# Ten of the sixteen S5 kernel matrices laid out in rows during the attention heads instead of during the S5

## The chip, the cores and the metric

One NeuronCore of a Trainium2 chip runs the whole program. The metric is device time in microseconds (us) of one execution, the median of several. Five engines work side by side, each through its own list of instructions and strictly in that list's order: TensorE (PE; PEld is its weight load), VectorE (DVE), ScalarE (ACT), GpSimd (POOL) and SyncE (SP). SP, ACT and POOL also issue DMAs, which share 16 DMA engines.

## The reference, cut to what matters

Two blocks on 256 tokens of width 1024: the first has an MLA attention layer and an S5 layer, the second two more attentions and a gated convolution. In the S5 layer 128 groups of 16 channels each pass through a linear recurrence, in both directions, over 256 context and 256 latent tokens:

```
def _s5_direction(u_ctx, u_lat, lam, dt, bmat, cmat):
    lam_bar = jnp.exp(lam * dt[:, None])
    b_bar = ((lam_bar - 1.0) / lam)[..., None] * bmat
    ...
        bu = jnp.einsum('btgs,gps->btgp', u_chunk.astype(jnp.complex64), b_bar)
        _, xs = lax.associative_scan(_ssm_combine, (a, bu), axis=1)
        xs = xs + powers[None] * h[:, None]
        y = jnp.einsum('btgp,gsp->btgs', xs, cmat).real
```

What a token contributes to the outputs of its own neighbourhood of four tokens depends on lam, dt, bmat and cmat alone, and not on the activations.

## The kernel before, in words

Tokens are taken in 64 steps of four. Within a step of four, the S5 is one small matrix per group (a 64 x 64 block-Toeplitz matrix, 4 tokens by 16 channels on either side); from step to step a state is carried. The 128 groups are worked in 16 sub-blocks of 8 (`m` or `sb`, 0 to 15).

**Ahead of the S5.** `s5_pre` makes three things of each sub-block from the parameters: BTd (input to state), CCd (state to output) and Kd, the distinct 16 x 16 blocks of the small matrices. All three go to DRAM. Sub-blocks 0 to 9 (`S5_EARLY = 10`) are made during the first projections (`region1`), 10 to 15 during the MLA output projection (`mla_out`). `s5_toeplitz` (L1127 to L1136) then copies Kd to Td, DRAM to DRAM, so that each row of a small matrix lies in one piece: 8 DMAs from the POOL queue, in pieces of 64 numbers (256 bytes).

**The S5 itself** (`s5`) follows a plan written by hand (`S5_PLAN`). Its first part is `sums`. For each sub-block m it projects the inputs of sub-block m + 2 (`inputs`; ACT copies them to `Ub` at L1178, writes them to DRAM as ud at L1179, POOL reads them back as `U` at L1185), and multiplies U with BTd on PE (`chunk_sums`, 64-partition matmuls, PSUM tiles `a`). ACT copies the products to `Sc` (L1214) and `s` (L1218). After every second sub-block DVE runs a tree over `Sc` (tiles `sc`, `Sc`), which gives the carried states of two sub-blocks, and between the trees the steps of a sequential scan (tiles `ss`, `s`). The tree of two sub-blocks is 24 DVE instructions, each scan 63 steps of three.

`direct(m)` is the part inside a step of four: SP loads the inputs (`Ul`, L1244) and the rows of the small matrices (`Ysb`, L1247, from Td; two buffers), ACT spreads Ysb into a zeroed matrix `x` (L1251, two copies; two such matrices, used in turn), and PE multiplies (`c` <- `Ul`, `x`, four matmuls of 64 columns). `outputs(m)` adds the part that comes from the states: ACT (or DVE) copies the states to `whi` (L1264 to L1271), PE multiplies into the same `c`. After every second sub-block ACT copies `c` to `Yb` (L1281) and writes it to DRAM as yd (L1282). `activate` reads four sub-blocks of yd back to `hl` (POOL, L1296), applies gelu (ACT, L1297), and `glu` multiplies by the first half of the GLU weights (PE, `a` <- `hl`, `raw`, L1311 loads). `gate` (PE, `b` <- `s`, `raw`; ACT, `sg`) is independent of the scans.

**What sets the order.** The program is written in Python, but a scheduler reorders it: it simulates the engines and puts each engine's instructions in an order of its own, within the dependences. A part written earlier, or made ready earlier, may move far. The list that results is fixed; on the chip each engine waits at its head.

The two places of the diff are `mla_heads`, which loops over the 16 heads, and `sums` in `s5`, where the Td writes are issued behind the read of U for m = 1 to 4:

```
if S5_LATE == 16 and m in TPM:
    with self.tc.issue_after(self.u_read):
        i = TPM.index(m)
        n = 8 // len(TPM)
        self.s5_toeplitz(0, 16, range(n * i, n * i + n))
```

Of the kernel before, what the change touches and what calls it, by code (L numbers as in the profile page):

```python
# [54 lines left out]
NR = 2  # L55
TPM = (1, 2, 3, 4)
TOEP = 0
ZGM = 6
PREM = (1, 1, 1, 1, 1, 1, 0, 0)
HLL = False  # L60
# [21 lines left out]
S5_EARLY = 10  # L82
# [125 lines left out]
class Builder:  # L208
# [380 lines left out]
    def mla_heads(self, rest):  # L589
# [48 lines left out]
        def scores(h):  # L638
            if h >= HM:
                return  # L640
            qa = st.pop(("qa", h))
            qf, qp = st.pop(("rot", h))
            pl = []

            def rotary(ps, x, q, keys, stop):

                self.mm(ps, x[:, q], self.kr[0][:, keys], False, False)
                self.mm(ps, x[:, q], self.kr[1][:, keys], False, stop)

            for tt in range(2):  # L650
                q = slice(tt * P, (tt + 1) * P)
                ps = self.ps("b")
                self.mm3(ps, two(qa, al, q), self.ckv, True, False)
                rotary(ps[:, lat], qp, q, lat, False)
                rotary(ps[:, cx], qf, q, cx, True)
                pl.append(self.softmax(att, ps, NT, MLA_SCALE, "pl", 4))
            ps = self.ps("b", (P, 2, NL))
            for tt in range(2):
                q = slice(NL + tt * P, NL + (tt + 1) * P)
                self.mm3(ps[:, tt], two(qa, al, q), two(self.ckv, al, cx), True, False)  # L660
                rotary(ps[:, tt], qf, q, cx, True)
            st["p", h] = pl, [self.softmax(att, ps[:, tt], NL, MLA_SCALE, "pc", 4) for tt in range(2)]

        def transposes(h):
            pl, pc = st.pop(("p", h))
            pt_l, pt_c = pair([P, 4, NL], "ptl", 1), pair([P, 2, NL], "ptc", 1)
            for b in range(2):
                pt = self.ps("c", (P, 2, 2, P))
                for k in range(2):
                    for tt in range(2):  # L670
                        nc.tensor.transpose(pt[:, k, tt], pl[tt][:, (2 * b + k) * P:(2 * b + k + 1) * P], self.ident)  # L671
                self.split(pt_l[0][:, 2 * b:2 * b + 2], pt_l[1][:, 2 * b:2 * b + 2], pt.rearrange("p k t q -> p k (t q)"))
            pt = self.ps("c", (P, 2, 2, P))
            for k in range(2):
                for tt in range(2):
                    nc.tensor.transpose(pt[:, k, tt], pc[tt][:, k * P:(k + 1) * P], self.ident)
            self.split(pt_c[0], pt_c[1], pt.rearrange("p k t q -> p k (t q)"))
            st["pt", h] = pt_l, pt_c

        def values(h):  # L680
            pt_l, pt_c = st.pop(("pt", h))
            po = self.ps("a")
            for k in range(4):
                self.mm3(po[:, lat], (self.V[0][:, k], self.V[1][:, k]), (pt_l[0][:, k], pt_l[1][:, k]), k == 0, k == 3)
            for k in range(2):
                self.mm3(po[:, cx], (self.V[0][:, 2 + k], self.V[1][:, 2 + k]), (pt_c[0][:, k], pt_c[1][:, k]), k == 0, k == 1)
            o = pair([P, NT], "o", 2)
            self.split(o[0], o[1], po)
            st["o", h] = o

        def outputs(h):
            if h < 0:
                return
            if h % 8 == 0:
                st["wuv"] = self.unit("w_uv", h // 8, 8, P)
                self.acts.append((self.s16([P, 8, NT], F32R), self.s16([P, 8, NT], F32R)))
            w = st["wuv"]
            pv = self.ps("a")
            self.mm3(pv, (w[0][:, h % 8], w[1][:, h % 8]), st.pop(("o", h)), True, True)
            g = self.gates[h // 8][:, h % 8]  # L700
            self.tt(g, pv, g, ALU.mult)
            a = self.acts[h // 8]
            self.split(a[0][:, h % 8], a[1][:, h % 8], g)
# [9 lines left out]
        for h in range(HM):  # L713
            scores(h + 1)
            if h == HM - 1 and FIRST_OUT == 0:
                self.out_first()
            transposes(h)
            queries(h + 2)
            if h == HM - 1 and FIRST_OUT == 1:
                self.out_first()  # L720
            values(h)
            outputs(h - 1)
            next(mods[h // 8])
        if FIRST_OUT == 2:
            self.out_first()
        outputs(HM - 1)
# [89 lines left out]
    def mla_out(self, pool):  # L816
# [18 lines left out]
        def scaled(kt):  # L835

            nc.scalar.activation(zG[:, kt, :NL], z[:, kt, :NL], AF.Copy, scale=G[:, kt, 0:1])
            nc.vector.tensor_scalar(zG[:, kt, NL:], z[:, kt, NL:], G[:, kt, 1:2], None, op0=ALU.mult)

        for m in range(KT):  # L840
# [10 lines left out]
            for _ in range(PREM[m]):  # L851
                next(bg, None)
            if m == ZGM:
                zG = self.s16([P, KT, NT])
                for kt in range(m):
                    scaled(kt)
            if m >= ZGM:
                scaled(m)
# [3 lines left out]
        zg = room.enter_context(pool("zg"))  # L862
        if TOEP:
            self.s5_toeplitz(0, TOEP)
        self.s5_steps(tmp)
# [273 lines left out]
    def s5(self):  # L1139
# [15 lines left out]
        def inputs(m, both=False):  # L1155

            if m in S5_SPLIT:
                ps = self.ps()
                if m == S5_SPLIT[0]:
                    hh.extend((self.s16([P, KT, NT], F32R), self.t(l1, [P, KT, NT], F32R, "hl", 1)))  # L1160
                    with self.tc.issue_after(self.h1_last):
                        for kt in range(KT):
                            x = self.split(hh[0][:, kt], hh[1][:, kt], self.h1[:, kt])
                    if HLL:
                        self.h_last = x
                self.linear(ps, "w_u", m, 1, KT, hh, al)
                place(m, ps)
            else:
                ms = range(m, m + 1 + both)
                ps = [self.ps() for _ in ms]  # L1170
                for x in self.linears32(ps, "w_u", ms, self.h1, al):
                    pass
                for i, p in zip(ms, ps):
                    place(i, p)
# [145 lines left out]
        def sums(m0, m1):  # L1320
            for m in range(m0, m1):
                if NR <= m + 2 < 16:
                    inputs(m + 2)
                for sb, at in LATE_AT:
                    if at == m:
                        if sb < 16:
                            next(bg)
                        else:
                            self.s5_toeplitz(TOEP, 16)
                if S5_LATE == 16 and m in TPM:  # L1330
                    with self.tc.issue_after(self.u_read):
                        i = TPM.index(m)
                        n = 8 // len(TPM)
                        self.s5_toeplitz(0, 16, range(n * i, n * i + n))
                yield from chunk_sums(m)

        def take(it, n=1):
# [3 lines left out]
        def turns(parts):  # L1341

            for k in range(3 * max([n for _, n in parts], default=0)):
                for blk, n in parts:
                    if k < 3 * n:
                        take(s[blk])
                        yield
# [16 lines left out]
        with ExitStack() as es:  # L1364
            for what, *x in S5_PLAN:
                if what == "order":
                    es.enter_context(self.in_order("p"))
                elif what in ("direct", "outputs", "gates", "y", "glu"):
                    if what == "y" and y32 is None:
                        y32 = self.t(l1, [P, 16, NL], F32, "hl", 1)  # L1370
                    if len(x) > 2:
                        glu(x[0], *x[2:])
                        continue
                    for m in range(*x):
                        dict(direct=direct, outputs=outputs, gates=gate, y=activate, glu=glu)[what](m)
                else:
                    steps = x[what == "sums":]
                    n, ops = turns(steps), 3 * sum(k for _, k in steps)
                    if what == "sums":
                        for i, _ in enumerate(sums(4 * x[0], 4 * x[0] + 4)):  # L1380
                            take(n, ops * (i + 1) // 48 - ops * i // 48)
                    take(n, 999)
# [475 lines left out]
```

## Time and profile before

| what | value |
| --- | --- |
| median of 3 runs | 1410.92 us (1406.25 to 1411.26) |
| profiled execution: its own time, its span | 1411.13 us, 1409.4 us |
| PE busy, DVE busy, ACT busy, POOL busy | 1346.1, 1056.6, 826.7, 88.6 us |
| mean granted TensorE clock | 0.981 |
| heads | about 160 to 380 us of the span |
| S5, `sums` to the first glu products | about 500 to 800 us |

The trace gives times from the start of the span. Each engine's timeline lists instructions with start and length, with runs of like ones merged; in square brackets stands how long the engine was idle before and what released it. PE's granted clock is a share of full speed: 1.00 is 2.4 GHz, 0.50 is 1.2 GHz. One matmul of four-byte numbers, such as those of `direct`, shows as two instructions on PE.

### The profile page before, as it was taken

The numbers are of one execution on the slowest core, as the hardware profiler recorded it, in microseconds if no ns is written. First come the engines' busy times: TensorE is split into PE (matmuls) and PEld (weight loads), VectorE is DVE, ScalarE is ACT, GpSimd is POOL, SyncE is SP. The second block draws the span as 40 slices with busy tenths as digits, with TensorE's granted clock in tenths as the row PEclk, the third lists the DMA queues.
The fourth block names the chain that finished last, engine by engine and source line by source line (L and its number), as shares of the span: only waits on it lengthen the run. The fifth ranks groups of instructions, "written<-read, shape, count | busy, mean of one in ns | idle before, by whom it ended". The sixth has DMA issues, their size and how long they took to land.

```text
span 1409.4 us, 26303 instructions
## 1 busy us (share of the span) xinstructions
PE 1346.1 (96%) x10034; PEld 1148.6 (81%) x10034; DVE 1056.6 (75%) x2552; ACT 826.7 (59%) x1441; POOL 88.6 (6%) x134
## 2 busy tenths in 40 slices
PE   6999999999999999896999999999999999999999
PEld 1677767877787667455877999999879999999999
DVE  5999578988699849899995565556657777688853
ACT  5798566665456843336577544445568654566642
POOL 1022000000111223110000000000100000000000
PEclk9999999999999989998999999999999999999999
DMA  9656434133375459563776766665433535566554
GB/s 365 203 175 234 138 130 144 42 129 133 99 256 184 145 163 316 169 193 100 236 213 203 248 212 191 193 187 187 148 105 120 159 121 159 180 181 183 187 186 134
DMA packets 96015, 248.40 MB, mean 176 GB/s; under 512 B 28208, under 2 KB 36784, under 8 KB 95504
## 3 DMA queue, kind: packets, MB, share of 16 engines
q1 hardware_dynamic: 70656, 204.50, 45.5%
q0 software_dynamic: 6576, 22.94, 5.0%
q10 hardware_dynamic: 18656, 19.27, 4.1%
q8 instruction: 79, 1.29, 0.4%
q14 instruction: 48, 0.39, 0.1%
HBM read 216.79 MB, written 31.98 MB: 177 GB/s over the span
## 4 chain that ended last, share of the span: by engine, by line
PE 70%; DVE 12%; ACT 8%; DMA 6%; issue 3%; ACTq 0%; SPq 0%; POOL 0%; POOLq 0%; DVEq 0%
PE a L228 58%; PE b L228 8%; DVE s L284 3%; DVE ss L284 2%; PE c L228 2%; DVE sc L284 2%; DVE Sc L284 2%; ACT whi L240 1%; PE c L671 1%; DVE wlo L284 1%; DMA raw<-in_w_up 1%; ACT zc L1102 1%; DMA Td<-Kd 1%; DMA s<-in_xT 1%; PE c L1093 1%
## 5 line engine op out<-in xcount | busy, mean ns | idle before, releaser
L228 PE MATMUL a<-s,whi 128*128 128x256 f32 (+2 forms) x3024 | 644.9, 310 | 3.8 <-ACT whi L240 3.8
L228 PEld LDWEIGHTS a<-s,whi 128*128 128x128 f32 x3024 | 493.5, 191 | 33.8 <-ACT whi L240 3.5
L228 PE MATMUL a<-s,wlo 128*128 128x256 f32 (+1 forms) x1512 | 464.3, 309 | 1.6 <-DVE wlo L284 1.5
L284 DVE TENSOR_TENSOR wlo<-raw,whi 128x1024 fp32r<-128x1024 f32 (+2 forms) x234 | 280.8, 1201 | 188.8 <-ACT whi L240 183.1
L240 ACT CAST whi<-raw 128x1024 fp32r<-128x1024 f32 (+2 forms) x234 | 240.5, 1031 | 248.0 <-PE a L228 176.9
L228 PEld LDWEIGHTS a<-s,wlo 128*128 128x128 f32 x1512 | 289.0, 191 | 15.9 <-DVE wlo L284 2.2
L228 PE MATMUL a<-s,raw 128*128 128x512 f32 (+2 forms) x272 | 105.1, 536 | 1.0 <-ACT s L1218 0.8
L284 DVE TENSOR_TENSOR bt<-x,bc 128x512 f32<-128x512 f32 x128 | 83.6, 692 | 9.8 <-DMA bc<-in_bc 8.5
L284 DVE TENSOR_TENSOR s<-s,ss 128x64 f32<-128x64 f32 x504 | 89.0, 221 | 2.7
L228 PEld LDWEIGHTS a<-s,raw 128*128 128x128 f32 x272 | 52.1, 196 | 43.6 <-issue 37.4
L228 PE MATMUL a<-x,whi 128*128 128x256 f32 (+1 forms) x384 | 74.2, 294 | 0.0
L228 PE MATMUL b<-s,raw 128*128 128x256 f32 x256 | 61.5, 397 | 3.7 <-ACT sg L1288 3.7
L284 DVE TENSOR_TENSOR ss<-x,s 128x128 f32<-128x128 f32 x248 | 63.4, 285 | 1.3
L228 PEld LDWEIGHTS a<-x,whi 128*128 128x128 f32 x384 | 60.4, 192 | 0.6
L228 PEld LDWEIGHTS b<-s,raw 128*128 128x128 f32 x256 | 49.8, 199 | 11.7 <-ACT sg L1288 4.2
L228 PE MATMUL a<-x,wlo 128*128 128x256 f32 (+1 forms) x192 | 56.1, 292 | 0.0
L284 DVE TENSOR_TENSOR sc<-LA,Sc 128x1024 f32<-128x1024 f32 (+5 forms) x96 | 44.4, 503 | 10.5 <-ACT Sc L1214 10.2
L1178 ACT COPY Ub<-a 128x512 f32<-128x512 f32 x14 | 8.2, 586 | 70.8 <-PE a L228 70.8
L733 DVE TENSOR_REDUCE st<-b 128x1 f32<-128x512 f32 (+1 forms) x64 | 34.8, 550 | 18.4 <-PE b L228 18.0
L284 DVE TENSOR_TENSOR Sc<-Sc,sc 128x1024 f32<-128x1024 f32 (+5 forms) x96 | 48.3, 503 | 0.4
L228 PEld LDWEIGHTS a<-U,whi 64*64 64x64 f32 x1024 | 30.8, 138 | 21.0 <-ACT s L1218 11.0
L228 PE MATMUL a<-U,whi 64*64 64x128 f32 x1024 | 35.0, 282 | 11.9 <-ACT s L1218 10.6
(382 smaller groups left out, 2277.7 us busy)
## 6 DMA issues: line engine op xcount, KB each, us to landing
raw<-in_w_glu SPq DMA_DIRECT2D x64, 512.0 KB, 3.5
raw<-in_w_up SPq DMA_DIRECT2D x42, 512.0 KB, 3.5
raw<-in_w_out SPq DMA_DIRECT2D x40, 512.0 KB, 3.6
raw<-in_wmod SPq DMA_DIRECT2D x32, 512.0 KB, 3.6
raw<-in_w_u SPq DMA_DIRECT2D x32, 512.0 KB, 4.0
s<-in_wmod SPq DMA_DIRECT2D x16, 512.0 KB, 8.0
raw<-in_w_in SPq DMA_DIRECT2D x16, 512.0 KB, 4.0
BTd<-BT ACTq DMA_DIRECT2D x16, 512.0 KB, 3.5
```

The source lines that it names most:

```text
L228: self.last = self.ins(self.nc.tensor.matmul(out, l, r, start=start, stop=stop))
L240: self.nc.scalar.copy(hi, src)
L284: return self.ins(self.nc.vector.tensor_tensor(out, a, b, op=op))
L671: nc.tensor.transpose(pt[:, k, tt], pl[tt][:, (2 * b + k) * P:(2 * b + k + 1) * P], self.ident)
L733: nc.vector.tensor_reduce(st[:, 0:1], ps, axis=AX.X, op=ALU.max)
L1093: nc.tensor.transpose(pt[:, e, ri], src, self.ident)
L1102: nc.scalar.copy(zt[f, :, 4:7], ct[f, :, 0:3])
L1178: nc.scalar.copy(u, ps.rearrange("p (r s c) -> p s r c", r=2, s=4))
```

## The change

The eight Td writes are issued twice: for the 10 early sub-blocks (40 of 64 pairs of groups), one write of each of the 8 row kinds in heads 3 to 10, and for the 6 late ones in the `sums` as before. Nothing is computed otherwise.

```
@@ -55,6 +55,7 @@
 TOEP = 0
+TOE_AT = 3
...
@@ -721,6 +722,8 @@
             values(h)
             outputs(h - 1)
             next(mods[h // 8])
+            if TOE_AT <= h < TOE_AT + 8:
+                self.s5_toeplitz(0, S5_EARLY, (h - TOE_AT,))
...
@@ -1331,7 +1334,7 @@
                         i = TPM.index(m)
                         n = 8 // len(TPM)
-                        self.s5_toeplitz(0, 16, range(n * i, n * i + n))
+                        self.s5_toeplitz(S5_EARLY, 16, range(n * i, n * i + n))
```

Up to the S5 the lists of PE, DVE, ACT and SP stay as they were. POOL has eight more instructions: all eight early writes stand together, behind POOL's last work on sub-block 9 and ahead of its first in `mla_out`.

From the S5's start the scheduler's order differs. `Ysb` of an early sub-block waits now for the early writes alone, and so the direct products of sub-blocks 0 to 5 move ahead. On PE those of sub-block 0 go into the projection of sub-block 2's inputs. Before, in the middle of that projection (`a_5331`):

```order
L228 MATMUL a_5331<-s_1103_5332,wlo_5353 128x512
L228 MATMUL a_5331<-s_1103_5332,whi_5352 128x512
L228 MATMUL a_5331<-hl_5333,whi_5352 128x512
L228 MATMUL a_5331<-s_1103_5332,wlo_5353 128x512
L228 MATMUL a_5331<-s_1103_5332,whi_5352 128x512
```

The same place of the change (there the projection is `a_5339`, the direct product `c_7274`):

```order
L229 MATMUL a_5339<-s_1103_5340,wlo_5361 128x512
L229 MATMUL a_5339<-s_1103_5340,whi_5360 128x512
L229 MATMUL c_7274<-Ul_7275,x_5328 128x64 x4
L229 MATMUL a_5339<-hl_5341,whi_5360 128x512
L229 MATMUL a_5339<-s_1103_5340,wlo_5361 128x512
L229 MATMUL a_5339<-s_1103_5340,whi_5360 128x512
```

The four direct matmuls stand behind the 13th of 24 matmuls of that projection. Behind the chunk sums of sub-blocks 0 to 5 stand two more each (sub-blocks 1, 2 and 3 in halves); before, such pairs stood behind the sums of sub-blocks 6 to 13.

On ACT the copies of three `Ysb` tiles move from there to the start of the S5. Before, between the last write of the first inputs and the copy of sub-block 2's:

```order
L904 ACTIVATE uo_5298<-u_5296,x_5243 128x4x64 x2
L905 DMA ud_92<-uo_5298 128x512
L1178 COPY Ub_5380<-a_5331 128x512
L1179 DMA ud_92<-Ub_5380 128x512
L1214 COPY Sc_5386<-a_5389 128x128x2
```

The same place of the change:

```order
L907 ACTIVATE uo_5306<-u_5304,x_5251 128x4x64 x2
L908 DMA ud_92<-uo_5306 128x512
L1254 COPY x_5328<-Ysb_7277 64x4x4x16 x2
L1254 COPY x_5329<-Ysb_7287 64x4x4x16 x2
L1254 COPY x_5328<-Ysb_7298 64x4x4x16 x2
L1181 COPY Ub_5388<-a_5339 128x512
L1182 DMA ud_92<-Ub_5388 128x512
```

Six copies stand now ahead of `Ub`; the last two can start only when PE has read `x_5328` in the first direct product.

Further on, the order changes where the states of sub-blocks 4 to 7 become outputs. On ACT, the end of `outputs(7)` before (`Yb_7829` holds sub-blocks 6 and 7; `sg` is a gate; the `Ysb` are those of sub-blocks 10 and 11):

```order
L1264 COPY whi_8268<-x_6279 64x16
L1265 COPY whi_8268<-x_6279 64x16
L1282 DMA yd_93<-Yb_7780 128x8x64
L1288 ACTIVATE sg_8212<-b_8201 128x256
L1289 DMA sgd_91<-sg_8212 128x256
L1281 COPY Yb_7829<-c_7601 128x512
L1264 COPY whi_8294<-x_6279 64x16
L1265 COPY whi_8294<-x_6279 64x16
L1282 DMA yd_93<-Yb_7829 128x8x64
L1251 COPY x_5320<-Ysb_7856 64x4x4x16 x2
L1251 COPY x_5321<-Ysb_7866 64x4x4x16 x2
```

The same place of the change:

```order
L1267 COPY whi_8276<-x_6287 64x16
L1268 COPY whi_8276<-x_6287 64x16
L1254 COPY x_5328<-Ysb_7864 64x4x4x16 x2
L1254 COPY x_5329<-Ysb_7874 64x4x4x16 x2
L1284 COPY Yb_7837<-c_7609 128x512
L1267 COPY whi_8302<-x_6287 64x16
L1268 COPY whi_8302<-x_6287 64x16
L1285 DMA yd_93<-Yb_7837 128x8x64
L1291 ACTIVATE sg_8220<-b_8209 128x256
```

The four copies of `Ysb` have changed places with `Yb`: they stand now ahead of it and of its write.

## Rows read from the trace of the kernel before

**Rows 1.** The page: shares of the chain of waits by engine.

```profile
PE 70%; DVE 12%; ACT 8%; DMA 6%; issue 3%; ACTq 0%; SPq 0%; POOL 0%; POOLq 0%; DVEq 0%
```

**Rows 2.** The chain of waits, 495 to 570 us: start, length, what.

```profile
554.36 8.78 DMA Td<-Kd
```

**Rows 3.** Timeline of PE, 561 to 589 us: start, length, instruction, idle before.

```profile
561.57 1.98 PE L228 MATMUL a<-U,whi 64*64 64x128 f32 x64
567.66 1.09 PE L228 MATMUL c<-Ul,x 128*128 128x64 f32 x4 [4.10 <-ACT x L1251]
569.57 9.41 PE L228 MATMUL a<-s,raw 128*128 128x512 f32 x16 [0.83 <-ACT s L1218]
578.91 1.98 PE L228 MATMUL a<-U,whi 64*64 64x128 f32 x64
580.82 0.66 PE L228 MATMUL c<-Ul,x 128*128 128x64 f32 x4
581.32 7.08 PE L228 MATMUL a<-s,raw 128*128 128x512 f32 x16
588.33 1.98 PE L228 MATMUL a<-U,whi 64*64 64x128 f32 x64
```

**Rows 4.** Busy time by stretch; after POOL: PEclk, DMA share, GB/s.

```profile
165.00:170.00 5.00, 5.00 (x24) 4.14 (x23) 3.02 (x6) 0.98 (x3) 0.00 (x0) 1.00 0.25 97
170.00:175.00 5.00, 5.00 (x24) 4.14 (x23) 1.39 (x2) 1.61 (x3) 0.00 (x0) 1.00 0.01 3
563.50:567.70 4.20, 0.10 (x5) 0.07 (x1) 4.20 (x17) 1.46 (x3) 0.00 (x0) 0.96 0.49 131
571.00:572.00 1.00, 1.00 (x2) 0.34 (x1) 0.86 (x5) 0.18 (x1) 0.25 (x1) 0.50 0.75 267
660.00:708.00 48.00, 44.35 (x317) 38.23 (x316) 48.00 (x264) 29.29 (x51) 0.75 (x1) 0.96 0.68 213
```

**Rows 5.** Timeline of DVE, 539 to 585 us.

```profile
539.00 2.36 DVE L284 TENSOR_TENSOR sc<-LA,Sc 128x1024 f32<-128x1024 f32 x2 [1.21 <-ACT Sc L1214]
...
582.14 2.36 DVE L284 TENSOR_TENSOR sc<-LA,Sc 128x1024 f32<-128x1024 f32 x2 [3.78 <-ACT Sc L1214]
```

**Rows 6.** Timeline of POOL around the heads.

```profile
158.72 0.24 POOL L1120 TENSOR_TENSOR Ks<-Ks,sk 128x32 f32<-128x32 f32 x1 [5.82 <-ACT Ks L1115]
...
383.41 0.57 POOL L822 DMA_DIRECT2D x<-FEd  x1 [224.44 <-PE a L228]
```

**Rows 7.** Timeline of PE at the S5's start.

```profile
509.47 0.40 PE L228 MATMUL a<-hl,whi 128*128 128x512 f32 x1
...
520.53 1.98 PE L228 MATMUL a<-U,whi 64*64 64x128 f32 x64
```

**Rows 8.** Timeline of SP at the S5's start.

```profile
503.44 5.40 SPq L1244 DMA_DIRECT2D Ul<-ud  x2
512.76 0.33 SPq L1201 DMA_DIRECT2D whi<-BTd  x1
```

**Rows 9.** The tile Ysb: copies and landing, min/median/max.

```profile
L1251 ACT COPY x<-Ysb x32: 644/658/689, 566.2 to 771.1; 64x256 f32<-64x256 f32 x32
...
DMA to landing us min/median/max: 2.0/3.6/5.7
```

**Rows 10.** Timeline of ACT: the S5's start, and around Yb.

```profile
513.01 0.58 ACT L1178 COPY Ub<-a 128x512 f32<-128x512 f32 x1 [8.09 <-PE a L228]
...
728.34 0.38 ACT L1288 ACTIVATE sg<-b 128x256 f32<-128x256 f32 x1
...
729.40 0.58 ACT L1281 COPY Yb<-c 128x512 f32<-128x512 f32 x1 [0.67 <-PE c L228]
...
730.46 2.70 ACT L1251 COPY x<-Ysb 64x256 f32<-64x256 f32 x4
```

**Rows 11.** Timeline of PE, 740 to 760 us.

```profile
743.41 4.15 PE L228 MATMUL a<-hl,raw 128*128 128x256 f32 x18 [0.77 <-ACT hl L1297]
750.29 8.86 PE L228 MATMUL a<-hl,raw 128*128 128x256 f32 x32 [2.73 <-DMA raw<-in_w_glu]
```

More of the change, by code (lines that the diff above doesn't have):

```diff
@@ L57 @@
 TOEP = 0
+TOE_AT = 3
 ZGM = 6
@@ L723, in mla_heads @@
             next(mods[h // 8])
+            if TOE_AT <= h < TOE_AT + 8:
+                self.s5_toeplitz(0, S5_EARLY, (h - TOE_AT,))
         if FIRST_OUT == 2:
@@ L1333, in sums @@
                         n = 8 // len(TPM)
-                        self.s5_toeplitz(0, 16, range(n * i, n * i + n))
+                        self.s5_toeplitz(S5_EARLY, 16, range(n * i, n * i + n))
                 yield from chunk_sums(m)
```

## The prediction

> **What bounds the kernel now.** I read the shares of the chain of waits first: PE has 70% of the chain, DVE 12%, DMA 6% [rows 1]. A change to DMAs can therefore pay only where a transfer stands in the chain, and the chain itself names such a place: one Td write of 8.78 us from 554.36 [rows 2], behind which Ysb is loaded. PE's timeline shows what that costs: at 567.66 the first direct product comes after 4.10 us of idle time, released by ACT's copies of Ysb; another 0.83 us follow, and then sixteen matmuls of a projection take 9.41 us, where the same sixteen take 7.08 us a period later [rows 3]. The granted clock says why: 0.50 at 571 to 572, against 0.96 just before the idle time [rows 4]. The disturbed period lasts from 561.57 to 578.91, 17.34 us; the next one, with as much work, from 578.91 to 588.33, 9.42 us. So the wait costs PE 17.34 - 9.42 = 7.92 us.
>
> Then DVE, since the same stretch feeds the scans. While PE idles, DVE is busy for 4.20 of 4.20 us, on the scan of the first unit and a tree. It waits for PE only at 582.14: 3.78 us until ACT delivers Sc. At 539.00, the tree before that but one, it waited 1.21 us for the same thing [rows 5]. From 660 to 708, in the second scan, DVE is busy for 48.00 of 48 us and PE for 44.35 [rows 4]. So in this part of the S5 PE sets the time up to 539, and DVE from there, with one gap of 3.78 us. What PE gains behind 539 counts only as far as DVE waited for it.
>
> **The change, part by part.**
>
> *Early writes, in the heads.* POOL does its last work before the heads at 158.72 and its next at 383.41, released by PE, with 224.44 us of idle time between [rows 6]. The eight new DMAs stand in that gap, all together. Eight writes, none with more data than that of 8.78 us [rows 2], end within 8 x 8.78 = 70 us even one after another, far ahead of their first reader at 503. On the 16 engines they meet a DMA share of 0.25 at 165 to 170 and of 0.01 at 170 to 175, with PE busy 5.00 of 5 us in both [rows 4]. I take 0. The cover is this free share; without it a weight load is held up by at most one transfer, 8.78 us, of which the heads' buffers take a part. Below nothing it can't be: nothing in the heads waits for Td.
>
> The Trainium skill ("DMA: Bandwidth & Descriptors", "Issuing engines are not separate DMA queues") says that DMAs started by different engines run on the same 16 DMA engines and interleave. By that rule a separate POOL queue protects nothing, and only the free share above does; it is why the collision is rival C.
>
> *Late writes, in the sums.* They keep their place and carry 24 of 64 columns of groups. DMA share there is 0.49 to 0.75 [rows 4]; less traffic can only help, and PE's periods there have no other DMA wait [rows 3]. 0.
>
> *The wait on the Td write.* It goes, since the first six direct products now depend on the early writes. PE gets back the 7.92 us, DVE 3.78, and what DVE waits for next is its own work. The Trainium skill ("TensorE: Matmul & The Clock Gate", Part 1) has the array throttled until activity releases it. The row at 571 agrees. Taken alone that rule counts the half-speed matmuls as a second gain, 9.41 - 7.08 = 2.33 us; but that is within the 7.92, and DVE's 3.78 is the limit for both.
>
> *Direct products ahead of the sums.* Two matmuls cost 0.50 us in the middle of PE's list (580.82 to 581.32) [rows 3]. Ahead of DVE's tree at 539.00 PE has now four for sub-block 0 and two each for three pairs of chunk sums, 10 x 0.25 = 2.5 us. They were done later before, where PE has 48.00 - 44.35 = 3.65 us of idle time in one stretch alone [rows 4], so their absence there gives nothing. DVE waited for PE at 539.00, so all of 2.5 us reaches it.
>
> *The first copy.* The first direct product stands where PE was at 509.47 [rows 7]. SP issues the load behind that of Ul at 503.44 [rows 8]; landing takes 2.0 to 5.7 us, median 3.6, and two copies 2 x 0.66 [rows 9]. From about 503.85 that is 507.2, 508.8 or 510.9: PE waits 0 to 1.4 us. I take 0.3, near the median.
>
> *Six copies ahead of Ub.* ACT idled 8.09 us before Ub at 513.01 [rows 10], room for four copies (2.6 us). The last two need the third tile's load and PE's first product. The second Ul's issue ends at 508.84 [rows 8]; with a landing of 3.6 us the second tile is there at 512.5, and four copies (two tiles) end at 515.1. Ub is due at 513.01 plus what PE is late, about 514.3. Sc and s stand behind Ub, so the delay of 0 to 1.8 us reaches DVE, though the chunk sums after it are PE's and catch up a part. I take 0.6.
>
> DVE is then late by 2.5 + 0.3 + 0.6 = 3.4 us at 539 and gets 3.78 back at 582: a gain of 0.4 us at the scan's end.
>
> *The tail.* ACT's four copies, 2.70 us, stood behind Yb at 729.40 and its write [rows 10]; now they stand ahead. Yb was copied at once when PE was done (idle 0.67 before it). The copies fill those 0.67 us first, and a gate's SiLU of 0.38 us, ahead of Yb until now, comes behind it [rows 10]. So Yb is 2.70 - 0.67 - 0.38 = 1.6 us later; bounds 0 and 2.70. Behind the write wait POOL's read of yd, gelu on ACT, and PE at 743.41 (0.77 us of waiting) [rows 11]. PE waits there already, so the delay passes on. At 750.29 PE waits 2.73 us for raw, whose buffer PE itself frees: no cover. So +1.6.
>
> **Sum.** -0.4 + 1.6 = +1.2 us. The profiled execution took 1411.13 us (span 1409.4), 0.2 above the median of 1410.92. So 1412.3 against it, 1412.1 as a median: **1412**. By the bounds: best -1.3 (shift 2.5, tail 0, all of 3.78 gained), worst 2.5 + 1.4 + 1.8 - 3.78 + 2.70 = +4.6, that is 1409.6 to 1415.5.
>
> **The rivals.**
>
> *A: PE's time counts, not DVE's.* The 7.92 us reach the end, because the gates and projections that PE does in those microseconds shorten the work behind the scan, or 3.78 + 1.21 = 5.0 us do, if the trees no longer wait at either place. 1403.0 to 1405.9. For it speaks PE's 70% of the chain [rows 1]; against it DVE's 48.00 of 48 us [rows 4] and the ten matmuls ahead of 539.
>
> *B: a new stall takes the place of the old one.* SP's list has five loads of Ysb, with two buffers, ahead of the BTd load that was issued at 512.76 [rows 8]. The fifth waits for the copies of the third, these for PE's first direct product. If BTd comes late for the chunk sums at 520.53 [rows 7], PE idles and its clock falls as it does now at 563: 4.10 + 2.33 = 6.4 us by rows 3, ahead of DVE's 539. Then 2.5 + 6.4 - 3.8 + 1.6 = +6.7, 1417.6. It decides from a Ysb landing of about 5.7 us on; the median is 3.6 [rows 9].
>
> *C: the early writes collide in the heads.* All eight stand together; the loads of the next heads share the engines. From a quarter to half of a transfer's 8.78 us then shows, +2 to +4, 1414 to 1416. Against it the share of 0.01 [rows 4].
>
> **How the numbers follow.** My forecast 0.65, A 0.15, B 0.12, C 0.08. A measurement here can tell about 0.5% from no change, 7 us: faster is below 1403.9, slower above 1418.0. A lies around the first bound on its far end, a third of it counts: 0.06 with what lies beyond. B lies just below the second, half of it counts: 0.06, and 0.01 from C. The rest is same: 0.87. The range takes in the forecast's own 1409.6 to 1415.5, C, B up to its price and the weaker form of A: 1405.5 to 1417.6.
>
> **What the profile after would show.** Right: no Td write in the chain; PE at the old 563 without idle time and at 1.00; DVE's first wait at 539 longer and later by about 3.4 us, none at 582 or under 1 us; the scan's end within 1 us of before; Yb and the first glu products 1 to 2 us late. In the heads PE's idle time as before. Wrong: PE waits over 2 us for x at 509 or for BTd at 520 (B); the scan ends 4 us or more earlier, or PE's work behind it is shorter by that (A); a wait for raw in the heads that was not there (C).

## The result, and the profile after

The change makes the kernel slower: 1419.89 us (four runs, 1419.11 to 1420.19) against 1409.49 us (four, the three known before and one of 1408.06), a ratio of 1.0075 with a 95% interval of 1.0051 to 1.0099. Seven runs of a second round gave 1416.82 us and a ratio of 1.0057 (1.0035 to 1.0080). The forecast was 1412, its range 1405.5 to 1417.6: the first median lies above the range, the second inside it. The profiled execution has a span of 1418.0 us, 8.6 more than before; that of the second round 1414.4.

The page's shares hardly move [rows 1]:

```profile
PE 72%; DVE 11%; ACT 8%; DMA 6%; issue 2%; ACTq 0%; SPq 0%; POOL 0%; DVEq 0%; POOLq 0%
```

So the places must be found. Four points of PE's timeline cut the stretch, and what lies between them can be compared between runs. A is PE's first product with `hl` in the projection of sub-block 2's inputs; B the last chunk sums, before which PE waits over 8 us; C the output products of sub-block 6 (`c` <- `whi`); D the first GLU product into a `b` tile. PE before, at B, between B and C, and at C:

```profile
654.31 4.23 PE L228 MATMUL a<-U,whi 64*64 64x128 f32 x64 [10.60 <-ACT s L1218]
...
669.66 5.41 PE L228 MATMUL b<-s,raw 128*128 128x256 f32 x16 [3.13 <-ACT sg L1288]
...
720.80 1.91 PE L228 MATMUL c<-whi,wlo 128*64 128x64 f32 x32 [2.76 <-ACT whi L1271]
```

PE after, from A on, the rows with a wait that matters:

```profile
505.69 0.51 PE L229 MATMUL a<-hl,whi 128*128 128x512 f32 x1 [2.07 <-DVE hl L285]
...
510.52 1.25 PE L229 MATMUL c<-Ul,x 128*128 128x64 f32 x8 [1.77 <-issue]
...
559.91 3.81 PE L229 MATMUL a<-U,whi 64*64 64x128 f32 x64 [3.99 <-DMA whi<-BTd]
...
655.96 4.22 PE L229 MATMUL a<-U,whi 64*64 64x128 f32 x64 [14.01 <-ACT s L1221]
...
670.50 9.43 PE L229 MATMUL b<-s,raw 128*128 128x256 f32 x32 [4.32 <-ACT sg L1291]
...
726.32 2.03 PE L229 MATMUL c<-whi,wlo 128*64 128x64 f32 x32 [2.77 <-ACT whi L1274]
...
751.58 4.15 PE L229 MATMUL a<-hl,raw 128*128 128x256 f32 x18 [2.40 <-ACT hl L1300]
758.59 7.17 PE L229 MATMUL a<-hl,raw 128*128 128x256 f32 x32 [2.86 <-DMA raw<-in_w_glu]
...
768.51 5.01 PE L229 MATMUL a<-hl,raw 128*128 128x256 f32 x22 [0.69 <-DMA raw<-in_w_glu]
```

The Td wait of [rows 3] is gone. In its place stand a first direct product that waits 1.77 us (the profile names no releaser; ACT's copies of its matrix ran from 509.10 to 510.41) and chunk sums that wait 3.99 us for BTd. The row behind B is the one that turned out to matter: the gates (`b` <- `s`, `raw`) wait 4.32 us for `sg`, and their first matmuls then run slowly (9.43 us for 32, where sixteen took 3.72 us undisturbed), at a granted clock of 0.50. In this view a stretch and its length are followed by the busy time of PE, PEld, DVE, ACT and POOL, then PE's granted clock, the DMA share and GB/s:

```profile
670.00:675.00 5.00, 4.50 (x11) 3.60 (x12) 5.00 (x12) 0.82 (x3) 0.00 (x0) 0.50 0.15 52
```

Between the points, in us (span times of the rows at A, B, C and D subtracted), with the runs of the experiments below:

| kernel | A to B | B to C | C to D | median | ratio (95%) |
| --- | --- | --- | --- | --- | --- |
| before | 149.28 | 66.49 | 64.67 | 1409.49 | |
| the change | 150.28 | 70.36 | 69.62 | 1419.89 | 1.0075 (1.0051 to 1.0099) |
| the change, again (e5) | 148.86 | 70.50 | 65.96 | 1416.82 | 1.0057 (1.0035 to 1.0080) |
| e1 writes in the heads only | 149.69 | 66.35 | 65.01 | 1410.20 | 1.0009 (0.9995 to 1.0024) |
| e2 early data, old places | 146.14 | 66.40 | 63.16 | 1407.15 | 0.9988 (0.9967 to 1.0010) |
| e11 the same, again | 146.47 | 65.48 | 62.73 | 1407.42 | 0.9984 (0.9964 to 1.0005) |
| e3 change, BTd first | 149.56 | 70.29 | 65.98 | 1414.62 | 1.0031 (1.0010 to 1.0051) |
| e4 change, gate first | 150.85 | 64.89 | 67.47 | 1410.9 | 1.0018 (0.9998 to 1.0038) |
| e6 change, both | 147.59 | 65.21 | 68.47 | 1410.46 | 1.0014 (0.9997 to 1.0032) |
| e7 change, first loads later | 148.05 | 64.62 | 66.00 | 1407.02 | 0.9985 (0.9974 to 0.9997) |
| e8 e2 and gate first | 145.40 | 64.97 | 64.90 | 1409.22 | 0.9990 (0.9972 to 1.0009) |
| e12 the same, again | 146.68 | 64.65 | 67.36 | 1409.86 | 0.9986 (0.9966 to 1.0006) |
| e9 e2 and gate late | 146.48 | 69.52 | 65.59 | 1411.10 | 1.0004 (0.9985 to 1.0022) |
| e10 before, gate first | 149.77 | 64.48 | 66.66 | 1409.83 | 0.9997 (0.9976 to 1.0018) |

A stretch comes from one profiled execution, a median from 4 to 12 runs, and the kernel before alone spread over 9.5 to 13.5 us in each round of experiments. Two of the 12 runs of e4 were slow (2183.64 and 4138.31 us); its median and its ratio are those of the other ten. In the first pair A lies 0.66 us later after than before, and A to B costs 1.00, B to C 3.87, C to D 4.95; behind D 1.8 us come back, which e5 does not repeat in size (0.85). Sum 0.66 + 1.00 + 3.87 + 4.95 - 1.8 = 8.7, the span's 8.6.

### The profile page after: what moved, and what is told of

It is laid out like the page before. It is cut to its first block, busy times and chain, and to the rows that moved or that the text cites. A ratio compares the mean times of both kernels' runs of the same rounds, so it can differ in the third digit from the quotient of the medians.

```text
span 1418.0 us, 26326 instructions
## 1 busy us (share of the span) xinstructions
PE 1345.7 (95%) x10034; PEld 1148.7 (81%) x10034; DVE 1056.0 (74%) x2552; ACT 827.0 (58%) x1441; POOL 92.3 (7%) x142
## 4 chain that ended last, share of the span: by engine, by line
PE 72%; DVE 11%; ACT 8%; DMA 6%; issue 2%; ACTq 0%; SPq 0%; POOL 0%; DVEq 0%; POOLq 0%
PE a L229 59%; PE b L229 9%; DVE s L285 2%; PE c L229 2%; DVE Sc L285 2%; DVE sc L285 2%; DVE ss L285 1%; DVE bt L285 1%; ACT whi L241 1%; DVE wlo L285 1%; ACT whi L1273 1%; DMA hl<-yd 1%; PE c L672 1%; ACT whi L1274 1%; DMA whi<-BTd 1%
## 5 line engine op out<-in xcount | busy, mean ns | idle before, releaser
L285 DVE TENSOR_TENSOR ss<-x,s 128x128 f32<-128x128 f32 x248 | 64.5, 283 | 1.2
```

The source lines that it names most:

```text
L285: return self.ins(self.nc.vector.tensor_tensor(out, a, b, op=op))
```

## The experiments

**e1. The writes alone.** To the kernel before only the early writes are added; the list of every other engine is the same.

```
             next(mods[h // 8])
+            if 3 <= h < 11:
+                self.s5_toeplitz(0, S5_EARLY, (h - 3,))
```

> The kernel before, with the eight early Td writes added in the heads and nothing else: all sixteen sub-blocks are written again in the sums as before, so no wait goes and the lists of PE, DVE, ACT and SP are those of before. Theory (the slowdown comes from the new order in the S5, not from the writes): no change, 1408 to 1412 us, heads with the same PE idle time within 1 us. Rival C (the writes collide with the heads' weight loads): 1413 us or more, with a wait of PE or ACT for a weight between 160 and 380 us.

Measured: 1410.20 us, ratio 1.0009. The heads, 160 to 380 us, of the kernel before:

```profile
160.00:380.00 220.00, 212.61 (x1320) 167.98 (x1319) 174.38 (x455) 129.00 (x285) 0.00 (x0) 0.99 0.33 108
```

and of e1:

```profile
160.00:380.00 220.00, 212.78 (x1329) 168.30 (x1328) 174.66 (x456) 129.55 (x285) 5.32 (x8) 1.00 0.36 116
```

The eight writes take POOL 5.32 us, raise the DMA share from 0.33 to 0.36, and PE does as much as before. Rival C falls.

**e2 (and e11). The early data without the new order.** SP's loads are held behind the BTd loads that they followed before (`bt[m]` is the load of sub-block m's BTd; `issue_after` fixes an order on one engine, it adds no wait):

```
+HU = {3: 10, 4: 12, 5: 14}
+HY = {0: 8, 1: 8, 2: 8, 3: 8, 4: 10, 5: 12, 6: 14}
...
+            with self.tc.issue_after(self.bt[HY[m]]) if m in HY else ExitStack():
+                nc.sync.dma_start(out=k, in_=self.Td[:, 4 * m:4 * m + 4])
```

(the same with `HU` for the load of `Ul`)

> The change, but the loads of Ysb and of the later Ul are held on SP behind the same BTd loads as in the kernel before, so that the direct products stand where they stood; only the wait for the Td write is gone. Theory: the 4.10 us of PE idle time at 563 go, DVE's wait of 3.78 us at 582 goes and nothing takes its place; 1404 to 1408 us. Rival (the loss is in the early or smaller writes, not in the order): as slow as the change, 1417 us or more. Rival (what DVE gets back is lost again further on, as in the change): 1409 to 1413 us.

Measured: 1407.15 us, A to B 3.1 us shorter. DVE's wait of 3.78 us [rows 5] became, in e2:

```profile
578.68 2.36 DVE L287 TENSOR_TENSOR sc<-LA,Sc 128x1024 f32<-128x1024 f32 x2 [0.69 <-ACT Sc L1220]
```

3.78 - 0.69 = 3.09, the 3.1 us. The bound that the prediction set for this gain was right, and the loss is in the order: DVE's list here is that of the kernel before. e11 repeated the kernel:

> The early data at the old places of the direct products once more, beside the next run on the same chip. Expected from the first time: 1406 to 1408.5 us, 2 to 3 us under the kernel before. If that was the spread of the runs: 1409 us or more.

It gave 1407.42 us. Both intervals still reach past 1.

**e3. BTd first.** In the change `HU` and `HY` hold the loads of sub-blocks 2 to 7 behind the next sub-block's BTd:

```
+HU = {m: m + 1 for m in range(2, 8)}
+HY = {m: m + 1 for m in range(2, 8)}
```

> The change, with the loads of Ul and Ysb of sub-blocks 2 to 7 held on SP behind the BTd load of the next sub-block. Sub-blocks 0 and 1 stay early; ACT's copy Yb of sub-blocks 6 and 7 then stands ahead of the copies of Ysb again, as in the kernel before. Theory (BTd of sub-block 5 was late because SP stood at the Ul of that sub-block; that and the tail are over half of the loss): PE's idle time of 3.99 us at 556 goes, DVE's third tree starts 3 to 4 us earlier, the gelu of sub-blocks 4 to 7 1 to 2 us earlier still; 1411 to 1415 us. Rival (DMA bandwidth in this stretch is the cause, any order of the loads leaves one late): PE waits over 2 us for another BTd or raw there, 1417 us or more.

Measured: 1414.62 us. Why BTd was late in the change stands in SP's timeline (L1247 loads `Ul`, L1204 BTd):

```profile
540.03 0.42 SPq L1204 DMA_DIRECT2D whi<-BTd  x1
548.22 0.37 SPq L1247 DMA_DIRECT2D Ul<-ud  x1
...
550.24 0.46 SPq L1204 DMA_DIRECT2D whi<-BTd  x1
551.41 4.64 SPq L1204 DMA_DIRECT2D whi<-BTd  x2
```

and in the chain of the change:

```profile
550.24 9.54 DMA whi<-BTd
```

SP stood from 540.45 to 548.22 at the `Ul` of sub-block 5, whose inputs were still being written (POOL's read of the same inputs waits for that write too, until 548.73), with BTd of the same sub-block behind it; released, SP issued seven loads within 4 us, and this one took 9.54 us to land (median 5.5 for the 15 loads of BTd from 500 to 640). The Trainium skill ("DMA: Bandwidth & Descriptors", "Issuing engines are not separate DMA queues") says that DMAs of all issuers share the same 16 engines and interleave; the 9.54 us agree, though no run here shows that the burst alone made it late. In e3 PE does not wait for BTd, yet the gain is small. PE waits for ACT instead:

```profile
551.78 1.18 PE L231 MATMUL a<-U,whi 64*64 64x128 f32 x28 [2.23 <-ACT Ub L1184]
```

and A to B is 149.56 us. So the late BTd was real, but taking its wait away did not shorten A to B, since another wait took its place. What e3 wins over the first run of the change lies behind C, where Yb stands ahead of the Ysb copies again: C to Yb takes 8.93 us in e3, 10.02 in the change, 10.06 in e5, 8.60 before. That Yb's place won it is not shown: e5, with Yb late, takes as long from C to D (65.96) as e3 (65.98).

**e4. Gate first.** In the change, ACT's copies `whi` of sub-block 2 are held behind the first gate's SiLU:

```
+SGH = {2: 0}
...
+            with self.tc.issue_after(self.sg[SGH[m]]) if m in SGH else ExitStack():
+                nc.scalar.copy(H[f, :, :, 0], C[f, :, g])
...
```

> The change, with ACT's four copies whi of sub-block 2 held behind the SiLU of the first gate, which in the change stands behind them. Theory (the gates' PSUM buffers are freed late, PE waits 4.32 us at 670 instead of 3.13 at 669 and passes 2.3 us on): PE starts the following gates 2 to 3 us earlier; 1417 to 1418.5 us. Rival (PE has slack in the second scan, as the prediction had it, and the gelu of sub-blocks 4 to 7 is not earlier): 1419.5 to 1420.5 us.

Measured: 1410.9 us, ratio 1.0018. More gain than expected: B to C falls from 70.36 to 64.89 us. Here is the place on ACT, in the kernel before:

```profile
660.39 1.28 ACT L1288 ACT_TABLE_LOAD   x1
661.68 0.38 ACT L1288 ACTIVATE sg<-b 128x256 f32<-128x256 f32 x1
...
669.22 0.38 ACT L1288 ACTIVATE sg<-b 128x256 f32<-128x256 f32 x1
```

in the change:

```profile
668.77 1.28 ACT L1291 ACT_TABLE_LOAD   x1
670.07 0.38 ACT L1291 ACTIVATE sg<-b 128x256 f32<-128x256 f32 x1
670.85 0.38 ACT L1291 ACTIVATE sg<-b 128x256 f32<-128x256 f32 x1 [0.40 <-ACT sg L1291]
```

and on PE, in e4:

```profile
665.25 3.72 PE L230 MATMUL b<-s,raw 128*128 128x256 f32 x16 [1.11 <-ACT sg L1294]
...
670.10 3.72 PE L230 MATMUL b<-s,raw 128*128 128x256 f32 x16 [0.76 <-ACT sg L1294]
...
719.95 1.64 PE L230 MATMUL c<-whi,wlo 128*64 128x64 f32 x32 [2.76 <-ACT whi L1277]
```

with the busy times there:

```profile
665.00:674.00 9.00, 7.99 (x42) 6.47 (x42) 9.00 (x34) 5.49 (x8) 0.00 (x0) 1.00 0.47 154
```

In the change the first SiLU starts 8.4 us later than before (6.7 us later counted from B). Until then it holds a PSUM tile `b` that PE's third gate needs. With the SiLU early, two waits of 1.11 and 0.76 us stand for the one of 4.32, and sixteen matmuls take 3.72 us: the clock stays at 1.00.

**e5. The change again.**

> The change itself once more, beside the next three on the same chip, since four runs of it stood against runs of the kernel before that spread over 10 us. Theory (the loss is in the order of instructions and so in every run): 1416 to 1420 us. Rival (a part of the 10 us was the runs' own spread): 1411 to 1415 us.

1416.82 us, with BTd 2.62 us late, the gates waiting 5.47 us and B to C at 70.50. The order's loss stands in both traces; about 3 us of the first 10 were spread. What differs most between them is C to D (69.62 and 65.96; its parts stand under what stays open).

**e6. Both edits.**

> The change with both edits at once: loads of Ul and Ysb of sub-blocks 2 to 7 behind the BTd load of the next sub-block (Yb of sub-blocks 6 and 7 then stands ahead of the Ysb copies), and the copies whi of sub-block 2 behind the first gate's SiLU. The first six products of sub-blocks 0 and 1 stay ahead of the trees. Theory (places add up: gates 4 to 5 us, Yb 1 to 2, BTd 1): 1407 to 1411 us. Rival (they hide one another, since one path takes over from the next): no better than the gate edit alone, 1412 to 1414 us.

1410.46 us: level with before. B to C 65.21, A to B 147.59; but C to D 68.47 us.

**e7. The first loads later.** Only `HY = {0: 3, 1: 3}`: the Ysb of sub-blocks 0 and 1 behind BTd of sub-block 3.

> The change with the loads of Ysb of sub-blocks 0 and 1 held on SP behind the BTd load of sub-block 3, so that no direct product stands ahead of the first two trees; the rest of the order follows from that (the first gate's SiLU and BTd of sub-block 5 stand about as in the kernel before). Theory (all of the loss hangs on the direct products being made as early as possible): no wait of PE at 510, the second tree at 539 as before, PE not idle for BTd; 1406 to 1410 us. Rival (early Ysb loads cost wherever they stand, by the DMA share of this stretch): 1413 us or more.

1407.02 us, ratio 0.9985 (0.9974 to 0.9997): two held loads take all of the loss away, since the scheduler's order behind them changes with them (the first SiLU, BTd of sub-block 5 and Yb stand about as before). The mechanism was not as expected at the front: the second tree starts 37.71 us behind A, as late as in the change (37.34), 33.97 before.

**e8 and e12. Early data and gate first.** e2 with `SGH`, and the first SiLU held behind the last copies of sub-block 15.

> The early data at the old places of the direct products (as in the run that held the loads), and the first gate's SiLU on ACT behind the last copies Sc and s of sub-block 15 and ahead of the copies whi of sub-block 2. Theory (in the run with the gate edit PE went from the last chunk sums to the outputs of sub-block 6 1.6 us faster than in the kernel before): PE's wait of 3.2 us at 666 falls under 1.5 and the clock stays up there; 1404 to 1407 us, 1 to 2 us under the run without it. Rival (only the order of the change needs this place): within 1 us of the run without it.

> Early data at the old places with the first gate's SiLU ahead of the copies whi of sub-block 2, once more, since its runs spread from 1400 to 1414 us. Theory (the traces show the two gains one after the other, 3 us until the last chunk sums and 1.5 us behind them): 1404 to 1407 us, under the run without the gate edit. Rival (the gates' gain is lost again behind the gelu): as the run without it, or 1409 us as the first time.

1409.22 and 1409.86 us: no better than e2, though B to C is shorter (64.97 and 64.65 against 66.40 and 65.48). The rival that e8's expectation names holds.

**e9. Gate late, without the change's order.** e2, with the first SiLU behind the copies `whi` of sub-block 2 (for this the plan names the copies of sub-blocks 0 to 2 ahead of the gates):

```
+            with self.tc.issue_after(self.ins(self.whi_last)) if m == 0 else ExitStack():
+                nc.scalar.activation(sg, ps, AF.Silu)
```

> The early data at the old places (as in the run that held the loads), but on ACT the first gate's SiLU stands behind the copies whi of sub-block 2, as it does in the change. Theory (this place alone makes the stretch from the last chunk sums to the products of sub-block 6 some 4 us longer, 70.4 us instead of 66.5): that stretch takes 69 to 72 us, PE waits over 4 us for sg once; 1410 to 1413 us, 3 to 5 us over the run without the edit. Rival (the stretch was longer in the change since PE and ACT came to it in another state): within 1 us of the run without the edit, 1406 to 1408 us.

1411.10 us, 3.7 to 4 over e2 and e11. PE in e9:

```profile
666.24 8.92 PE L231 MATMUL b<-s,raw 128*128 128x256 f32 x32 [5.42 <-ACT sg L1305]
...
721.30 2.03 PE L231 MATMUL c<-whi,wlo 128*64 128x64 f32 x32 [2.75 <-ACT whi L1297]
```

The wait of the change is made by hand in a kernel without its order, and B to C is 69.52. With e4, e6, e8, e10 and e12 (64.5 to 65.2) this one place on ACT decides the stretch both ways. In e10 no other computation on ACT changes its place; in e9 a few later ones do.

**e10. Gate first in the kernel before.**

> The kernel before with the gate edit alone: the first gate's SiLU behind the copies Sc and s of sub-block 15 and ahead of whi of sub-block 2. No early writes, nothing else. Theory: the stretch from the last chunk sums to the products of sub-block 6 takes 65.0 us instead of 66.5, also here; 1407 to 1409 us. Rival (the gain needs the early data): 1409 to 1411 us.

1409.83 us, although B to C fell to 64.48. What was won is lost ahead of D. PE in e10:

```profile
775.08 0.50 PE L229 MATMUL a<-s,whi 128*128 128x256 f32 x2 [0.81 <-ACT whi L241]
776.58 1.17 PE L229 MATMUL c<-whi,wlo 128*64 128x64 f32 x32 [0.99 <-DMA wlo<-CCd]
```

and its busy times there, PEclk and DMA share behind POOL:

```profile
770.00:775.00 5.00, 4.27 (x95) 3.93 (x94) 2.10 (x2) 2.04 (x4) 0.75 (x1) 1.00 0.98 349
775.00:780.00 5.00, 3.93 (x45) 3.69 (x46) 3.11 (x5) 3.93 (x9) 0.00 (x0) 0.77 0.73 216
```

A load (`wlo`) that was in time before now lands 0.99 us after PE is ready for it, and the granted clock falls to a mean of 0.77. The DMA engines are full (0.98), but they were so before (1.04 from 770 to 775), where PE came here 3.0 us later. The kernel before, the same five microseconds:

```profile
775.00:780.00 5.00, 4.19 (x101) 3.78 (x101) 2.75 (x3) 2.21 (x3) 0.00 (x0) 1.00 0.94 326
```

## Why the prediction was wrong

**The step that failed** is in what bounds the kernel: "PE sets the time up to 539, and DVE from there". DVE is indeed busy without a gap: 67.00 of 67 us from 654 to 721, before

```profile
654.00:721.00 67.00, 59.83 (x486) 51.75 (x488) 67.00 (x362) 47.58 (x69) 0.75 (x1) 0.93 0.65 203
```

and after

```profile
654.00:721.00 67.00, 59.44 (x441) 51.38 (x443) 67.00 (x353) 43.85 (x68) 0.75 (x1) 0.89 0.57 180
```

But what C needs of DVE was ready earlier. The way to C begins with ACT's copies `whi` for sub-block 4 (six copies of about 2 us, then C), and these need the last step of the scan of sub-blocks 4 to 7. By the counts of `S5_PLAN` its first instruction is number 163 of DVE's 252 `ss` instructions. Here are this step and the first copy, in the kernel before and in the change:

```profile
704.00 0.48 DVE L284 TENSOR_TENSOR ss<-x,s 128x128 f32<-128x128 f32 x2
708.82 1.97 ACT L1270 COPY whi<-s 64x1008 f32<-64x1008 f32 x1
...
706.85 0.48 DVE L285 TENSOR_TENSOR ss<-x,s 128x128 f32<-128x128 f32 x2
714.34 1.99 ACT L1273 COPY whi<-s 64x1008 f32<-64x1008 f32 x1 [0.40 <-DVE s L285]
```

The step takes some 0.8 us, so ACT's copies came 4 us after it before and 6.7 in the change. The bracket names DVE only since the profile infers a releaser from the last semaphore event; ACT was issuing a write from 713.97. For the same reason the chain of the kernel before seems to run along DVE up to 708.82. In e4 and e7 the copies come 1.3 and 0.4 us after the step, so DVE is the next bound there and not far off.

C moves with ACT's place for one SiLU while DVE's list stays the same: 66.40 and 69.52 us behind B in e2 and e9, 70.36 and 64.89 in the change and e4. A full engine was taken for the bound of its stretch; what bounds B to C is PE, with ACT, through the two `b` tiles of the gates. Up to B the step holds: B follows ACT's first copies `whi`, which DVE's scan released at 648.37 before and at 651.28 after. The Trainium skill ("Perfetto Trace Analysis", "Identifying the Most-Contended Engine") names the engine of highest occupancy as the one to improve first; from B to C the runs differ from it. So the moved SiLU was not in the sum at all, though the order showed it; B to C is 3.87 and 4.01 us longer in the two traces of the change, and e4, which undoes it, has a median 6 us under the second round of the change and 9 under the first (ratios to before: 1.0018 against 1.0057 and 1.0075).

**Point by point.**

- *Early writes, 0*: right (e1). Rival C is out.
- *Td wait gone, DVE gains at most 3.78*: right, and only where the old order stays: behind A the fourth tree starts 2.4 to 3.7 us earlier in e2, e8, e9, e11 and e12 (73.40 to 74.70 us, before 77.11).
- *Ten matmuls, first copy and Ub, 3.4 us at the second tree*: right in sum: 37.34 and 37.42 us behind A, 33.97 before, so 3.37 and 3.45. The first wait was 1.77 us, above its bound of 1.4.
- *What DVE waits for next is its own work*: wrong. The third tree waited for BTd, in the change:

```profile
543.02 2.36 DVE L285 TENSOR_TENSOR sc<-LA,Sc 128x1024 f32<-128x1024 f32 x2 [2.04 <-ACT Sc L1217]
...
564.71 2.36 DVE L285 TENSOR_TENSOR sc<-LA,Sc 128x1024 f32<-128x1024 f32 x2 [2.88 <-ACT Sc L1217]
```

  ACT's `Sc` came late in the second of these rows since PE had waited for BTd. That is the mechanism of rival B (SP's head blocked, BTd late), at sub-block 5 instead of 1 and by a load of `Ul` instead of Ysb. The third tree starts 7.2 us later behind A than before (59.03 against 51.85), of which 3.8 is the stall.
- *A gain of 0.4 at the scan's end*: A to B came out at +1.00 and -0.42, near the forecast, by two errors that cancel: the stall, and some 2 us that came back between the fourth tree and B (72.17 us before, 69.85 after). 1.27 of these are ACT's copies of one Ysb, which stood among its copies ahead of B (648.37 to 653.61 before, 651.28 to 655.25 after) and which the sum had left out; the rest was not traced.
- *The tail, 1.6*: Yb is 1.4 us later behind C (10.02 and 10.06 against 8.60), right. But behind it the delay reached the gelu whole in one trace and hardly in the other (C to the products with `hl`: 22.61 us before, 25.26 in the change, 22.89 in e5), by the DMA from yd to `hl` (6.08 us against 4.53 in the chain).
- *Behind the gelu, nothing more*: wrong by 1.0 to 2.3 us. In all five traces with the change's order (the change, e3 to e6) PE waits there for raw (0.59 to 0.77 us), `Ul` (1.02 to 1.26) and DVE's `wlo` (0.75), which it does not before; in the first of them the DMA share is 0.83 and 1.01 at the two loads.
- *Rival A*: out in the change; with the old order the medians of e2 and e11 lie 2.4 us under the kernel before, which their intervals do not tell from nothing.

**What stays open.** C to D takes from 62.7 to 69.6 us. Its parts can be read, here for the kernel before, the change, e5 and e12:

```profile
720.80:785.47 64.67, 60.35 (x576) 53.16 (x577) 45.34 (x189) 46.34 (x66) 1.50 (x2) 0.95 0.68 211
...
726.32:795.94 69.62, 60.07 (x577) 53.31 (x577) 42.93 (x172) 46.47 (x66) 1.50 (x2) 0.95 0.65 203
...
725.42:791.38 65.96, 58.67 (x577) 51.71 (x577) 42.75 (x171) 46.38 (x66) 1.50 (x2) 0.97 0.68 213
...
716.85:784.21 67.36, 62.22 (x576) 55.20 (x577) 48.16 (x200) 46.40 (x66) 1.50 (x2) 0.91 0.71 216
```

Take from PE's busy time what the lower clock cost it (an estimate: the length times one minus the granted clock), and 56.2 to 57.2 us are left in all fourteen traces. What differs is PE's idle time and the clock. Idle are 7.0 to 9.6 us in the five traces with the change's order, 7.0 in e7 and 3.8 to 5.5 in the others, so the order costs some 3 us and more here too. e5 waits more than the kernel before (7.3 against 4.3 us) and has a short C to D only because its clock stood higher. e8, e10 and e12 lose to the clock (0.91 to 0.93) what the early gate won.

Why the clock falls in one trace and not in another stays open, and the 0.66 us at A in the first pair have no cause shown. The spread of single runs goes with the clock: of the 35 runs of the kernel before beside e1 the fastest (1402.83 us) has a mean granted clock of 0.988, the slowest (1416.35) of 0.976.

## What to carry to other kernels

An edit that makes data ready earlier hands a reordering scheduler a new problem: read the new order on every engine through the end of the stage, and price each instruction that changed places, most of all those that free a buffer (a SiLU that empties a PSUM tile). An engine that is busy all the time bounds a stretch only if the next stage waits for what it makes in that stretch; count off which of its instructions that is, since a releaser in a profile is inferred. Here holding two loads back kept the early data and took the loss away; the gain that was left is about 0.15%, which these runs tell from nothing only once (e7, with an upper bound of 0.9997); one interval of so many can miss 1 by luck.

## What the runs showed of the hardware

Idle times of 1 to 5 us on PE can cost more than their length, as the granted clock falls from 1.00 (2.4 GHz) to 0.50 (1.2 GHz), but not each time. Behind 4.32 and 5.42 us of waiting 32 gate matmuls took 9.43 and 8.92 us (0.50 from 670 to 675 in the change); behind 1.11 us sixteen took 3.72 us at 1.00. In e10 waits of 0.81 and 0.99 us, with a start at 775.08 and 776.58, were followed by 0.50 from 777.7 to 780; before, a wait of 0.81 us at 778.12 left 1.00. The Trainium skill ("TensorE: Matmul & The Clock Gate", Part 1) has activity release the throttle; that waits of about 1 us end differently shows that the length of one wait does not tell.

Over the whole program the runs of e5 have a mean granted clock of 0.977, those of the kernel before beside them 0.981. By an estimate (0.004 of 1417 us) up to 5.7 us of the change's loss stand in time at the lower clock.

A load can land late in a burst: BTd took 9.54 us as one of seven loads that SP issued within 4 us, against a median of 5.5 us for BTd from 500 to 640. That the burst is the cause was not tested.
